# Mixture of experts: ranking the experts right behind the router's mask, and spreading the 64-slot blocks among the 128-slot blocks

## The chip, the cores and the metric

The kernel runs on one core of a Trainium2 chip. The metric is the device time in microseconds of one execution. One execution was recorded by the hardware profiler; times inside it are counted from the start of its span.

## The reference

The model is a chain of three blocks on a sequence of 256 tokens with 1024 channels, all in float32. What comes last, and takes almost half of the time, is the feed-forward part of the third block, a mixture of 8 experts of which each token uses two:

```python
def moe_swiglu(h, router, we_gate, we_up, we_down):
    logits = (h @ router).astype(jnp.float32)
    top_v, top_i = lax.top_k(logits, TOP_K)
    top_w = jax.nn.softmax(top_v, axis=-1)
    gates = jnp.sum(jax.nn.one_hot(top_i, N_EXPERTS, dtype=jnp.float32) * top_w[..., None], axis=-2)
    out = jnp.zeros_like(h)
    for e in range(N_EXPERTS):
        out = out + gates[..., e:e + 1] * swiglu(h, we_gate[e], we_up[e], we_down[e])
    return out
```

`swiglu` is `(silu(h @ w_gate) * (h @ w_up)) @ w_down`, with 1024 x 3584 for gate and up and 3584 x 1024 for down. Three float32 matrices for each of 8 experts are 352 MB, and every one is read from HBM once. The result is added to the residual stream x, which is the kernel's output. The two blocks before, and the attention of the third, are untouched by the change.

## The kernel before

**Slots.** The kernel doesn't run all 256 tokens through each expert. It has eight places for experts, numbered by `KINDS`, with a fixed number of slots each: the places 0, 2 and 4 (kind F) have 128, the places 1, 3, 5, 6 and 7 (kind N) have 64. `route` (from L1310) computes the logits, finds each token's two experts, and builds `mask` (L1354), a 0/1 matrix of tokens by experts. Two sums over it follow on TensorE: `pos` (L1362, L1363), each token's position in its expert's queue, and `cnt` (L1398, L1399, in `count`), each expert's number of tokens. `one_hots` (L1477, four instructions) compares positions with slot numbers and so makes the selection matrix `sel` of a group, and `gather` (L1500) multiplies the tokens by it, so that the chosen tokens stand in the slots. For kind F the operands are split into a high and a low part (`hth`, `htl`, L268 and L269), for three matmuls with rounded operands instead of one in full float32.

**Ranking.** `order` ranks experts 1 to 7 by count on VectorE, and so decides which expert takes which place: the fullest get 128 slots. Place 0 is always expert 0. It writes `ids` as integers into `self.ci` (L1427), the largest overflow likewise (L1433), and the positions `spos` sorted by place (L1441 and L1442 in `sort`). SyncE loads the ids into registers (L1644, `values_load`), because the address of a weight tile depends on them; it loads the overflow (L1646), which says at the end whether a second round is needed. With the inputs here none is run.

**Blocks.** Each expert's 3584 hidden channels are worked on in 7 blocks of 512. A block loads six tiles of 1 MB: two of gate, two of up, two of down. All loads are issued by SyncE in the order of the program, each into a buffer of a ring: 10 buffers and 2 more, and 3 further ones until the third block. A load has to wait until the tile that was in its buffer has been read. In a block of kind F each tile is split by ScalarE (`whi`, L305) and VectorE (`wlo`, L306) in two halves of 1024 columns, into four buffers of each, and is free when that is done, and TensorE runs 24 matmuls of 512 columns for each of gate, up and down (L1566, L1589). In a block of kind N the raw tile goes to TensorE in float32 (L1558, 16 matmuls of 256 columns for each of gate and up; L1577, 8 of 512 for down), and is free when those have run. The down part of a block is run behind the gate and up parts of the next. After an expert's last block, `combine` scales its result (`yh` on ScalarE, `yl` on VectorE, L1678 and L1679), multiplies by the transposed selection (`cmb`), and adds to x on VectorE: 8 additions of 128 x 256 for N (L1688), 4 of 128 x 512 for F (L914). The program (`experts`, from L1592) makes a list `seq` of 56 blocks; before, with e0 to e7 the places, it is

- F F, then N F nineteen times, then N sixteen times.

The gather for the next group of `GROUPS` stands two or three blocks ahead of its first block. Within the engines a scheduler may move instructions by priority; each engine then runs its own list in order.

Of the kernel before, what the change touches and what calls it, by code (L numbers as in the profile page):

```python
# [24 lines left out]
SWA_ORDER = [0, 3, 1, 4, 2, 5, 6, 9, 7, 10, 8, 11]  # L25
CAP = {"F": 128, "N": 64}
KINDS = "FNFNFNNN"
GROUPS = ((0,), (1,), (2, 3), (4, 5), (6,), (7,))
TAGS = ("u", "u", "x2", "u", "x2", "u")
HEAD = 2  # L30
PE_TAPS = 13
EARLY = 7
# [3 lines left out]
AHEAD = 3  # L36
# [172 lines left out]
class Build:  # L209
# [1102 lines left out]
    def route(self):  # L1312

        nc = self.nc
        t = self.units(4, "hn")
        self.ht = []
        after = self.after  # L1320
        acc = self.sum_sq(self.x[:3], fold=False)
        with self.tc.high_priority(offset=400):
            pl = self.pa("router")
            for j in range(4):
                for c in range(2):
                    g = self.col("swf_g", 2 * j + c)
                    if (j, c) == (3, 1):
                        nc.vector.tensor_scalar(t[j][:, c, :], self.x[j][:, c, :], g, None, op0=OP.mult)
                    else:
                        hn = nc.scalar.activation(t[j][:, c, :], self.x[j][:, c, :], AF.Copy, scale=g)  # L1330
                for c in range(2):
                    cc = 2 * j + c
                    for tb in range(2):
                        mm = nc.tensor.matmul(pl[:, tb * 8:(tb + 1) * 8], t[j][:, c, tb * 128:(tb + 1) * 128],
                                              self.col("router", cc * 8, 8), start=cc == 0 and tb == 0, stop=cc == 7,
                                              skip_group_check=True)
            rt = self.cpool.tile([128, 160], F32, name="rt")
            two = lambda o, w: rt[:, o:o + 2 * w].rearrange("p (a b) -> p a b", a=2)
            first = lambda m, k: m[:, :, k:k + 1].to_broadcast([128, 2, 8])
            lg, mx, ixf = rt[:, 0:16], two(16, 8), two(32, 8)  # L1340
            mask, tmp, pos = rt[:, 48:64], two(64, 8), rt[:, 80:96]
            ix = self.mpool.tile([128, 16], U32, name="ix", tag="m")
            nc.vector.tensor_copy(lg, pl[:, 0:16])
            for tb in range(2):
                s = slice(tb * 8, tb * 8 + 8)
                nc.vector.max(mx[:, tb, :], lg[:, s])
                nc.vector.max_index(ix[:, s], mx[:, tb, :], lg[:, s])
            nc.vector.tensor_copy(rt[:, 32:48], ix)
            iota = self.con("iota", 0, 8).rearrange("p (a b) -> p a b", a=1).to_broadcast([128, 2, 8])
            hot = two(112, 8)  # L1350
            m3 = mask.rearrange("p (a b) -> p a b", a=2)
            nc.vector.tensor_tensor(hot, iota, first(ixf, 0), op=OP.is_equal)
            nc.vector.tensor_tensor(tmp, iota, first(ixf, 1), op=OP.is_equal)
            masked = nc.vector.tensor_tensor(m3, hot, tmp, op=OP.add)  # L1354
            pt = []
            with after(mm):
                for j in range(4):
                    pt.append(self.turn(t[j], "PSSP"[j]))
            for j in range(HT0):
                self.turned(pt[j], masked, hn)  # L1360
            pp = self.pa("pos")
            nc.tensor.matmul(pp[:, 0:16], self.con("before"), mask, start=True, stop=False, skip_group_check=True)  # L1362
            nc.tensor.matmul(pp[:, 8:16], self.con("one").to_broadcast([128, 128]), mask[:, 0:8], start=False, stop=True,  # L1363
                             skip_group_check=True)
            nc.vector.scalar_tensor_tensor(pos, pp[:, 0:16], 1.0, mask, op0=OP.add, op1=OP.mult)
            self.pos, self.rt = pos, rt
            self.count()
            sel = self.one_hots(0, 0)
            for j in range(HT0, 4):
                self.turned(pt[j], self.hots, hn)  # L1370
            nxt = self.gather(0, sel, tags="ASP")
            self.order()
        with after(*self.gathered):
            rc = self.rms_col(self.sum_sq(self.x[3:], acc=acc))
            d, gw = two(96, 1), two(98, 2)
            nc.vector.tensor_tensor(d, mx[:, :, 1:2], mx[:, :, 0:1], op=OP.subtract)
            nc.vector.tensor_tensor(d, d, rc.rearrange("p (a b) -> p a b", a=2), op=OP.mult)
            nc.scalar.activation(gw[:, :, 1:2], d, AF.Exp)
            nc.vector.tensor_scalar(d, gw[:, :, 1:2], 1.0, None, op0=OP.add)
            nc.vector.reciprocal(gw[:, :, 0:1], d)  # L1380
            nc.vector.tensor_tensor(gw[:, :, 1:2], gw[:, :, 1:2], gw[:, :, 0:1], op=OP.mult)
            nc.vector.tensor_tensor(hot, hot, first(gw, 0), op=OP.mult)
            nc.vector.tensor_tensor(tmp, tmp, first(gw, 1), op=OP.mult)
            gates = two(128, 9)
            nc.vector.tensor_tensor(gates[:, :, 0:8], hot, tmp, op=OP.add)
            nc.vector.tensor_copy(gates[:, :, 8:9], rc.rearrange("p (a b) -> p a b", a=2))
            self.gates = gates
        for tb in range(2):
            self.sort(self.sgates[:, tb, 0:8], gates[:, tb, 0:8])
        nc.vector.tensor_copy(self.sgates[:, :, 8:9], gates[:, :, 8:9])  # L1390
        return nxt
# [9 lines left out]
    def order(self):  # L1401


        nc = self.nc
        pc = self.pc
        so = self.unit("so").rearrange("p a b -> p (a b)")
        cnt, key, rank = so[:, 0:8], so[:, 8:16], so[:, 16:24]
# [13 lines left out]
        nc.vector.tensor_tensor(P, each(so[:, 202:210], 8), row(rank, 8), op=OP.is_equal)  # L1421

        self.order_of = P, t
        ids, over = so[:, 186:194], so[:, 194:202]
        self.sort(ids, self.con("iota", 0, 8))
        self.ci = so[:, 211:220].bitcast(I32)
        nc.vector.tensor_copy(self.ci[:, 0:8], ids)  # L1427
        self.sort(over, cnt)
        ends = over.rearrange("p (a b) -> p a b", b=2)
        nc.vector.tensor_scalar(ends[:, 0:3, 0:1], ends[:, 0:3, 0:1], float(CAP["N"] - CAP["F"]), None, op0=OP.add)  # L1430
        nc.vector.tensor_reduce(so[:, 210:211], over, axis=AX.X, op=OP.max)
# [49 lines left out]
    def gather(self, g, sel, tag="u", tags="A"):  # L1481

        nc = self.nc
        kinds = [KINDS[e] for e in GROUPS[g]]
        xe = {}
# [106 lines left out]
    def experts(self, rnd, nxt):  # L1592


        nc = self.nc
        blocks = {k: [(e, b) for e in range(8) if KINDS[e] == k for b in range(7)] for k in "FN"}
        seq = blocks["F"][:HEAD]
        for n, f in zip(blocks["N"], blocks["F"][HEAD:]):
            seq += [n, f]
        seq += blocks["N"][len(blocks["F"]) - HEAD:]  # L1600
        at = {group[0]: g for g, group in enumerate(GROUPS)}
        early = {seq.index((group[0], 0)) - (2 if g == 1 else AHEAD): g for g, group in enumerate(GROUPS) if g}
        back, state, xes, yps, done = {}, {0: nxt}, {}, {}, None
        last, self.queued = None, []
        if rnd == 0:
# [1 line left out]
        for i, (e, b) in enumerate(seq):  # L1607
# [31 lines left out]
            if i in early:  # L1639
                g = early[i]  # L1640
# [75 lines left out]
```

## Time and profile before

| | us |
|---|---|
| median of 3 runs (lowest, highest) | 1842.62 (1842.45, 1848.72) |
| profiled execution, its own time | 1842.34 |
| its span | 1840.6 |
| TensorE busy (share of the span) | 1777.9 (97%) |
| VectorE busy | 1105.8 (60%) |
| ScalarE busy | 876.8 (48%) |
| mean DMA rate | 289 GB/s |

The span begins with the first instruction and ends with the last; the execution's own time is 1.7 us longer. The shares are means over stages that differ much: the routing starts at about 983 us, the first expert's matmuls at 995.9 us, the last load lands at about 1827 us. The page's chain of waits names only the final addition into x (L1688), so that what bounds the end has to be read from windows and timelines of the stages.

### The profile page before, as it was taken

What the parts mean: (1) busy time and instruction counts of PE and PEld (TensorE: products, weight loads), DVE (VectorE), ACT (ScalarE), POOL (GpSimd) and SP (SyncE); (2) the same over time, 40 slices, a digit from 0 to 9 for tenths busy, and PEclk for the clock granted to TensorE, in tenths of its full rate; (3) what the DMA queues carried; (4) which work ended last, traced back from release to release, by engine and by line L of the source; (5) the groups of instructions that cost most, each with busy time, mean ns of one, the idle gap of its engine ahead of it and who ended that gap; (6) DMA issues with size and microseconds to landing.
All of it is one profiled execution on the core that took longest, in us unless ns stands there. A gap on an engine that the chain in (4) does not pass through costs nothing. (4 is left out here: it accounts for less than half of the span.)

```text
span 1840.6 us, 30697 instructions
## 1 busy us (share of the span) xinstructions
PE 1777.9 (97%) x12370; PEld 1449.9 (79%) x12370; DVE 1105.8 (60%) x1730; ACT 876.8 (48%) x1345; POOL 11.4 (1%) x31
## 2 busy tenths in 40 slices
PE   7999999999999999999999999999999999999886
PEld 7989999989999979999978766666676667655432
DVE  7689788766467977665687754566565646420100
ACT  5545555555455675454576644545454545410000
POOL 0000000000000000000000000000000000000000
PEclk9999999999999999999998999999999999999999
DMA  9766468445554315555635899999999999999997
GB/s 307 250 247 229 166 233 296 149 150 198 191 185 165 115 46 196 191 176 180 244 115 196 353 397 420 420 415 418 421 421 414 416 408 420 420 420 420 421 420 298
DMA packets 77654, 531.30 MB, mean 289 GB/s; under 512 B 9282, under 2 KB 10050, under 8 KB 15424
## 3 DMA queue, kind: packets, MB, share of 16 engines
q1 hardware_dynamic: 75168, 524.66, 72.9%
q0 software_dynamic: 1328, 3.29, 0.9%
q8 instruction: 99, 1.62, 0.4%
q10 hardware_dynamic: 1008, 1.31, 0.2%
q14 instruction: 51, 0.42, 0.1%
HBM read 526.60 MB, written 2.62 MB: 288 GB/s over the span
## 5 line engine op out<-in xcount | busy, mean ns | idle before, releaser
L306 DVE TENSOR_TENSOR wlo<-raw,whi 128x1024 fp32r<-128x1024 f32 (+1 forms) x534 | 630.4, 1203 | 288.9 <-ACT whi L305 287.1
L305 ACT ACTIVATE whi<-raw 128x1024 fp32r<-128x1024 f32 (+1 forms) x534 | 543.3, 1040 | 355.1 <-PE lin L325 236.5
L325 PE MATMUL lin<-hh,whi 128*128 128x256 f32 x1248 | 355.6, 285 | 10.3 <-ACT whi L305 8.1
L325 PE MATMUL lin<-hl,whi 128*128 128x256 f32 x1248 | 354.3, 284 | 0.3
L325 PE MATMUL lin<-hh,wlo 128*128 128x256 f32 x1248 | 352.7, 283 | 1.8 <-DVE wlo L306 1.8
L325 PEld LDWEIGHTS lin<-hh,whi 128*128 128x128 f32 x1248 | 237.7, 191 | 14.5 <-ACT whi L305 9.1
L325 PEld LDWEIGHTS lin<-hh,wlo 128*128 128x128 f32 x1248 | 237.2, 190 | 4.7 <-DVE wlo L306 2.5
L325 PEld LDWEIGHTS lin<-hl,whi 128*128 128x128 f32 x1248 | 237.8, 191 | 2.4 <-issue 1.0
L1577 PE MATMUL y<-raw,an 128*64 128x512 f32 x560 | 131.3, 600 | 9.5 <-DMA raw<-we_down 9.0
L1558 PE MATMUL up<-raw,xn 128*64 128x256 f32 x1120 | 130.6, 381 | 9.3 <-DMA raw<-we_up 5.5
L1636 DVE SCALAR_TENSOR_TENSOR act<-up,gs,act 128x256 f32<-128x256 f32 (+1 forms) x56 | 32.6, 583 | 173.1 <-PE up L1558 142.0
L1558 PE MATMUL g<-raw,xn 128*64 128x256 f32 x1120 | 130.8, 383 | 5.8 <-DMA raw<-we_gate 5.8
L1558 PEld LDWEIGHTS up<-raw,xn 128*64 128x64 f32 x1120 | 80.0, 137 | 54.0 <-ACT act L289 8.2
L1558 PEld LDWEIGHTS g<-raw,xn 128*64 128x64 f32 x1120 | 76.6, 137 | 49.6 <-DMA raw<-we_gate 10.8
L1566 PE MATMUL g<-whi,xe 128*128 128x512 f32 x336 | 106.4, 398 | 0.0
L1566 PE MATMUL up<-whi,xe 128*128 128x512 f32 x336 | 104.7, 393 | 0.0
L1577 PEld LDWEIGHTS y<-raw,an 128*64 128x64 f32 x560 | 37.2, 136 | 82.7 <-issue 64.2
L289 ACT ACTIVATE act<-g,gs 128x256 f32<-128x256 f32 (+1 forms) x56 | 31.0, 554 | 126.2 <-PE g L1558 106.1
L1665 ACT ACTIVATE an<-aT 128x256 f32<-128x256 f32 x35 | 13.4, 382 | 146.5 <-PE aT L1662 146.5
L1566 PEld LDWEIGHTS up<-whi,xe 128*128 128x128 f32 x336 | 63.2, 188 | 13.9
L325 PE MATMUL ff<-fl,whi 128*128 128x256 f32 x256 | 71.8, 281 | 0.0
L325 PE MATMUL ff<-fh,wlo 128*128 128x256 f32 x256 | 71.8, 281 | 0.0
(457 smaller groups left out, 3082.6 us busy)
## 6 DMA issues: line engine op xcount, KB each, us to landing
raw<-we_gate SPq DMA_DIRECT2D x112, 1024.0 KB, 11.5
raw<-we_up SPq DMA_DIRECT2D x112, 1024.0 KB, 12.0
raw<-we_down SPq DMA_DIRECT2D x112, 1024.0 KB, 12.5
raw<-w_in SPq DMA_DIRECT2D x35, 1024.0 KB, 6.2
raw<-w_ff SPq DMA_DIRECT2D x32, 1024.0 KB, 4.9
raw<-ada_w SPq DMA_DIRECT2D x24, 1024.0 KB, 5.3
raw<-cv_w_gate SPq DMA_DIRECT2D x11, 1024.0 KB, 4.8
raw<-cv_w_up SPq DMA_DIRECT2D x11, 1024.0 KB, 4.8
```

The lines of the kernel that those rows point to most:

```text
L289: self.last_gate = self.nc.scalar.activation(*args, **kw)
L305: self.splits_done.append(nc.scalar.activation(hi[:, :w], raw[:, o:o + w], AF.Copy))
L306: self.low_done = nc.vector.tensor_tensor(lo[:, :w], raw[:, o:o + w], hi[:, :w].bitcast(F32), op=OP.subtract)
L325: nc.tensor.matmul(o, s, m, start=start and n == 0, stop=stop and n == 2, skip_group_check=True)
L1558: nc.tensor.matmul(ps[64 * h:64 * h + 64, 0:256], xe["N"][:, kk, :], raw[:, k * 512 + h * 256:k * 512 + (h + 1) * 256], start=kk == 0, sto ...
L1566: nc.tensor.matmul(ps, s, m, start=n == 0, stop=n == 23)
L1577: self.downs = nc.tensor.matmul(yp[0][64 * n:64 * n + 64, :], st, raw[:, k * 1024 + n * 512:k * 1024 + (n + 1) * 512], start=b == 0 and pa ...
L1636: nc.vector.scalar_tensor_tensor(t, pu[:, 0:w], gs[1], t, op0=OP.mult, op1=OP.mult)
L1665: nc.scalar.activation(an[:, 0:256], pt[:, 0:256], AF.Copy)
```

## The change

`route` now calls `count` and `order` right behind the mask, ahead of the transposes of the tokens and of the matmuls for `pos`. The second half of `order` becomes `overflow`: the sort of the counts, the largest overflow, and the sorts of the positions (`spos`); it is called behind the first `gather`. In `experts` the list of blocks is now made by spreading the 19 F blocks that follow the first two evenly over 35 N blocks:

- F F, then sixteen times N N F and three times N F among them, the last of these at the end. The last block is so of kind F (e4); before it was N (e7).

Place 5 is now gathered before and apart from place 4, which makes one more gather in all; a group is gathered ahead of whichever of its experts comes first in the list.

```diff
--- before.py
+++ after.py
@@ -25,8 +25,8 @@
 SWA_ORDER = [0, 3, 1, 4, 2, 5, 6, 9, 7, 10, 8, 11]
 CAP = {"F": 128, "N": 64}
 KINDS = "FNFNFNNN"
-GROUPS = ((0,), (1,), (2, 3), (4, 5), (6,), (7,))
-TAGS = ("u", "u", "x2", "u", "x2", "u")
+GROUPS = ((0,), (1,), (2, 3), (5,), (4,), (6,), (7,))
+TAGS = ("u", "u", "x2", "u", "u", "x2", "u")
 HEAD = 2
 PE_TAPS = 13
 EARLY = 7
@@ -1352,6 +1352,9 @@
             nc.vector.tensor_tensor(hot, iota, first(ixf, 0), op=OP.is_equal)
             nc.vector.tensor_tensor(tmp, iota, first(ixf, 1), op=OP.is_equal)
             masked = nc.vector.tensor_tensor(m3, hot, tmp, op=OP.add)
+            self.rt = rt
+            self.count()
+            self.order()
             pt = []
             with after(mm):
                 for j in range(4):
@@ -1363,13 +1366,12 @@
             nc.tensor.matmul(pp[:, 8:16], self.con("one").to_broadcast([128, 128]), mask[:, 0:8], start=False, stop=True,
                              skip_group_check=True)
             nc.vector.scalar_tensor_tensor(pos, pp[:, 0:16], 1.0, mask, op0=OP.add, op1=OP.mult)
-            self.pos, self.rt = pos, rt
-            self.count()
+            self.pos = pos
             sel = self.one_hots(0, 0)
             for j in range(HT0, 4):
                 self.turned(pt[j], self.hots, hn)
             nxt = self.gather(0, sel, tags="ASP")
-            self.order()
+            self.overflow()
         with after(*self.gathered):
             rc = self.rms_col(self.sum_sq(self.x[3:], acc=acc))
             d, gw = two(96, 1), two(98, 2)
@@ -1421,11 +1423,16 @@
         nc.vector.tensor_tensor(P, each(so[:, 202:210], 8), row(rank, 8), op=OP.is_equal)
 
         self.order_of = P, t
-        ids, over = so[:, 186:194], so[:, 194:202]
+        self.so, ids = so, so[:, 186:194]
         self.sort(ids, self.con("iota", 0, 8))
         self.ci = so[:, 211:220].bitcast(I32)
         nc.vector.tensor_copy(self.ci[:, 0:8], ids)
-        self.sort(over, cnt)
+
+    def overflow(self):
+
+        nc = self.nc
+        so, over = self.so, self.so[:, 194:202]
+        self.sort(over, so[:, 0:8])
         ends = over.rearrange("p (a b) -> p a b", b=2)
         nc.vector.tensor_scalar(ends[:, 0:3, 0:1], ends[:, 0:3, 0:1], float(CAP["N"] - CAP["F"]), None, op0=OP.add)
         nc.vector.tensor_reduce(so[:, 210:211], over, axis=AX.X, op=OP.max)
@@ -1595,11 +1602,16 @@
         nc = self.nc
         blocks = {k: [(e, b) for e in range(8) if KINDS[e] == k for b in range(7)] for k in "FN"}
         seq = blocks["F"][:HEAD]
-        for n, f in zip(blocks["N"], blocks["F"][HEAD:]):
-            seq += [n, f]
-        seq += blocks["N"][len(blocks["F"]) - HEAD:]
-        at = {group[0]: g for g, group in enumerate(GROUPS)}
-        early = {seq.index((group[0], 0)) - (2 if g == 1 else AHEAD): g for g, group in enumerate(GROUPS) if g}
+        rest = blocks["F"][HEAD:]
+        for n, block in enumerate(blocks["N"]):
+            seq.append(block)
+            k = len(rest) * (n + 1) // len(blocks["N"]) - len(rest) * n // len(blocks["N"])
+            seq += rest[len(seq) - n - 1 - HEAD:][:k]
+        assert len(seq) == 56
+        at = {}
+        for g, group in enumerate(GROUPS):
+            at[min(group, key=lambda e: seq.index((e, 0)))] = g
+        early = {seq.index((e, 0)) - (2 if g == 1 else AHEAD): g for e, g in at.items() if g}
         back, state, xes, yps, done = {}, {0: nxt}, {}, {}, None
         last, self.queued = None, []
         if rnd == 0:
```

The order of VectorE's instructions between the mask (L1354) and the gather. `cnt`, `pos` are the sums, `so` holds all of the ranking, `sel` is the selection, `htl` the low part of the transposed tokens, `xe` the gathered ones. Before:

```order
L1354 TENSOR_TENSOR rt<-rt 128x16
L269 TENSOR_TENSOR htl<-ht,hth 128x512
L1365 SCALAR_TENSOR_TENSOR rt<-pos,rt 128x16
L1477 TENSOR_SCALAR sel<-consts,rt 128x128 x4
L269 TENSOR_TENSOR htl<-ht,hth 128x512 x3
L1510 CAST xe<-xe 128x256 x3
L1410 COPY so<-cnt 128x8
```

And now, from the row behind the mask on:

```order
L1412 COPY so<-cnt 128x8
L1368 SCALAR_TENSOR_TENSOR rt<-pos,rt 128x16
L1413 SCALAR_TENSOR_TENSOR so<-so,consts 128x8
L1417 TENSOR_TENSOR so<-so 128x7x7
L269 TENSOR_TENSOR htl<-ht,hth 128x512
L1419 TENSOR_REDUCE so<-so 128x7
L1484 TENSOR_SCALAR sel<-consts,rt 128x128
L1423 TENSOR_TENSOR so<-so 128x64
L1484 TENSOR_SCALAR sel<-consts,rt 128x128
L1448 TENSOR_TENSOR so<-so,consts 128x64
L1484 TENSOR_SCALAR sel<-consts,rt 128x128
L1449 TENSOR_REDUCE so<-so 128x8
```

The fourth `sel` and the conversion of the ids (L1429) come next, and then three `htl`. Ranking and selection now stand interleaved, where the ranking stood behind three of the gather's conversions; on TensorE the two matmuls of `cnt` have changed places with those of `pos`.

SyncE's queue around the first load of the ids (L1644 before, L1656 now); `raw` is a tile of weights. Before:

```order
L281 DMA raw<-we_up 128x2048 x2
L281 DMA raw<-we_down 128x2048 x3
L281 DMA raw<-we_gate 128x2048
L1644 TENSOR_LOAD so
L1644 ISA x2
```

And now:

```order
L281 DMA raw<-we_up 128x2048 x2
L281 DMA raw<-we_down 128x2048 x3
L1656 TENSOR_LOAD so
L1656 ISA x2
L281 ISA
```

One load of gate, which belonged to the fourth block (expert 0, whose address is known) stood ahead of the ids; the fourth block is now of kind N, and its loads come behind.

VectorE's last rows; `al` is the low part of the activations, `cmb` the combined result. Before:

```order
L1636 SCALAR_TENSOR_TENSOR act<-up,gs,act 128x256 x5
L1679 SCALAR_TENSOR_TENSOR yl<-y_16641,gs,yh 128x512
L1688 TENSOR_TENSOR x<-x,cmb 128x256 x8
L1646 TENSOR_LOAD so
L1303 COMPARE_AND_BRANCH
```

And now:

```order
L306 TENSOR_TENSOR wlo<-raw,whi 128x1024 x8
L1648 SCALAR_TENSOR_TENSOR act<-up,gs,act 128x512
L1691 SCALAR_TENSOR_TENSOR yl<-y_16041,gs,yh 128x512
L1681 TENSOR_TENSOR al<-aT,ah 128x512
L1700 TENSOR_TENSOR x<-x,cmb 128x256 x8
L306 TENSOR_TENSOR wlo<-raw,whi 128x1024 x4
L1691 SCALAR_TENSOR_TENSOR yl<-y_15279,gs,yh 128x512
L914 TENSOR_TENSOR x<-x,cmb 128x512 x2
L1691 SCALAR_TENSOR_TENSOR yl<-y_15280,gs,yh 128x512
L914 TENSOR_TENSOR x<-x,cmb 128x512 x2
```

The list ended with one result to scale and eight additions; it now ends with those of e7, the splits of the last two down tiles of e4 behind them, and then the two results of e4 with four additions of twice the size.

## Rows read from the trace of the kernel before

**Rows 1.** The second part of the page: the span in 40 slices of 46 us, one digit or number per slice. Busy tenths of TensorE, and GB/s moved.

```profile
PE   7999999999999999999999999999999999999886
GB/s 307 250 247 229 166 233 296 149 150 198 191 185 165 115 46 196 191 176 180 244 115 196 353 397 420 420 415 418 421 421 414 416 408 420 420 420 420 421 420 298
```

**Rows 2.** Busy time by window. Columns: the window in us from the span's start, its length, busy us of PE, PEld, DVE, ACT and POOL with the number of instructions in brackets, granted TensorE clock (1.00 is 2.4 GHz, 0.50 is 1.2 GHz), DMA share, GB/s. First four stages in order, then three short windows inside the third.

```profile
984.00:1000.00 16.00, 16.00 (x84) 15.31 (x84) 10.69 (x43) 7.05 (x14) 0.52 (x1) 0.68 0.20 67
1032.00:1064.00 32.00, 32.00 (x192) 21.88 (x190) 19.05 (x22) 15.57 (x19) 0.53 (x1) 1.00 0.80 293
1064.00:1600.00 536.00, 532.37 (x2977) 368.96 (x2972) 301.29 (x326) 254.42 (x315) 1.58 (x3) 1.00 1.01 417
1600.00:1816.00 216.00, 193.64 (x1366) 103.24 (x1366) 25.04 (x51) 22.46 (x48) 0.00 (x0) 1.00 1.01 420
1208.00:1216.00 8.00, 8.00 (x60) 4.21 (x58) 1.10 (x2) 1.40 (x3) 0.00 (x0) 1.00 0.98 386
1414.00:1434.00 20.00, 20.00 (x122) 12.29 (x122) 10.56 (x14) 7.24 (x9) 0.00 (x0) 1.00 0.98 393
1478.00:1490.00 12.00, 12.00 (x85) 6.75 (x85) 2.67 (x4) 2.84 (x4) 0.00 (x0) 1.00 0.98 369
```

**Rows 3.** Who SyncE's DMA queue waited for: first between 976 and 1004 us, then (behind the dots) between 1195 and 1210 us. Total us, times, longest.

```profile
SPq L1644 <- DVE so L1441: 13.8, 1, 13.8
...
SPq L281 <- DVE wlo L306: 10.6, 3, 5.3
```

**Rows 4.** Timeline of the DMA issues on SyncE's queue. Columns: start, us until the last issue of the row has been made, line, tile and source, number of issues.

```profile
984.36 0.33 SPq L281 DMA_DIRECT2D raw<-we_gate  x1
999.43 0.90 SPq L281 DMA_DIRECT2D raw<-we_gate  x2
1044.53 3.08 SPq L281 DMA_DIRECT2D raw<-we_gate  x2
1050.23 3.11 SPq L281 DMA_DIRECT2D raw<-we_up  x2
1058.36 2.06 SPq L281 DMA_DIRECT2D raw<-we_down  x2
1062.54 0.91 SPq L281 DMA_DIRECT2D raw<-we_gate  x2
```

**Rows 5.** Timeline of TensorE: the first gate matmuls of a 128-slot block (L1566), and of the 64-slot blocks of two later pairs (L1558). Columns: start, us, line, tiles, shapes, number.

```profile
1045.04 0.71 PE L1566 MATMUL g<-whi,xe 128*128 128x512 f32 x2
1088.87 3.67 PE L1558 MATMUL g<-raw,xn 128*64 128x256 f32 x32
1117.19 1.08 PE L1558 MATMUL g<-raw,xn 128*64 128x256 f32 x8
```

**Rows 6.** Timeline around the router's mask and the ranking, VectorE first, then TensorE. Columns as in rows 5; in square brackets the idle time before and what ended it.

```profile
986.35 0.17 DVE L1354 TENSOR_TENSOR rt<-rt 128x16 f32<-128x16 f32 x1
989.18 0.17 DVE L1365 SCALAR_TENSOR_TENSOR rt<-pos,rt 128x16 f32<-128x16 f32 x1 [1.89 <-PE pos L1363]
989.40 0.87 DVE L1477 TENSOR_SCALAR sel<-consts,rt 128x128 fp32r<-128x128 f32 x4
995.49 0.15 DVE L1410 COPY so<-cnt 128x8 f32<-128x8 f32 x1
997.93 0.22 DVE L1442 TENSOR_REDUCE so<-so 128x8 f32<-128x64 f32 x1
998.19 0.17 DVE L1427 CAST so<-so 128x8 int32<-128x8 f32 x1
988.29 0.45 PE L1362 MATMUL pos<-rt,consts 128*128 128x16 f32 x2
989.43 0.57 PE L1399 MATMUL cnt<-rt,consts 128*128 128x8 f32 x2
995.89 0.63 PE L1566 MATMUL g<-whi,xe 128*128 128x512 f32 x2
```

**Rows 7.** Busy time by windows of 1 us around the routing; columns as in rows 2.

```profile
982.00:983.00 1.00, 0.04 (x1) 0.00 (x0) 0.89 (x2) 0.98 (x2) 0.00 (x0) 1.00 0.00 0
984.00:985.00 1.00, 1.00 (x7) 1.00 (x7) 0.34 (x1) 0.00 (x0) 0.00 (x0) 0.51 0.00 0
994.00:995.00 1.00, 1.00 (x9) 1.00 (x9) 0.42 (x1) 0.32 (x2) 0.00 (x0) 0.87 0.00 0
995.00:996.00 1.00, 1.00 (x10) 1.00 (x10) 0.85 (x7) 0.72 (x4) 0.00 (x0) 1.00 0.08 16
```

**Rows 8.** Timeline of the end of the span: the last down matmuls, the two halves of the scaled result, and the eight additions into x.

```profile
1827.29 1.94 PE L1577 MATMUL y<-raw,an 128*64 128x512 f32 x8 [0.17 <-DMA raw<-we_down]
1829.27 0.69 ACT L1678 ACTIVATE yh<-y,gs 128x512 fp32r<-128x512 f32 x1 [4.14 <-PE y L1577]
1829.99 0.75 DVE L1679 SCALAR_TENSOR_TENSOR yl<-y,gs,yh 128x512 fp32r<-128x512 f32 x1 [10.09 <-ACT yh L1678]
1831.33 2.74 DVE L1688 TENSOR_TENSOR x<-x,cmb 128x256 f32<-128x256 f32 x8 [0.59 <-PE cmb L1684]
```

**Rows 9.** Groups of instructions by line and shape between 1064 and 1620 us: count | busy us, mean ns of one | idle time before, and what ended it.

```profile
L306 DVE TENSOR_TENSOR wlo<-raw,whi 128x1024 fp32r<-128x1024 f32 x216 | 253.1, 1222 | 98.2 <-ACT whi L305 97.3
L914 DVE TENSOR_TENSOR x<-x,cmb 128x512 f32<-128x512 f32 x8 | 5.3, 682 | 2.0 <-PE cmb L1695 2.0
```

## The prediction

> **What bounds the kernel now.** I read the page's slices first, then windows by stage, then SyncE's waits and issues, since the page's chain ends at once. In the slices the last eighteen move about 420 GB/s whatever TensorE does [rows 1]. The windows say the same by stage: 417 GB/s from 1064 to 1600 us, while TensorE is busy 532 of 536 us, and 420 from 1600 to 1816, while it is idle 216.0 - 193.6 = 22.4 us [rows 2]. The reader is to see that 420 is a ceiling: the rate is no higher where TensorE waits for data. A load of 1 MB (1.049 MB decimal) is then 2.5 us, six for a block 15.0 us. What can be gained in the experts is DMA time below 420, and it lies in three places: a gap at 984 to 1000 us (67 GB/s), 1032 to 1064 (293), and some dips behind 1064 [rows 2].
>
> The gap has a named cause: SyncE waits 13.8 us for the ranking before it can address expert place 1 [rows 3], between the issues at 984.4 and 999.4 us [rows 4]. The second shortage and the dips are waits for ring buffers: the loads issued from 1044.5 on come one by one as buffers come free [rows 4], and during the dip at 1208 SyncE waited for splits, at most 5.3 us at a time [rows 3]. TensorE meanwhile never stops. An N-F pair takes it 1117.19 - 1088.87 = 28.3 us [rows 5]; an N block is three parts of 3.67 us and a transpose, 11.3, so an F block is 17.0. So at the start TensorE is behind the loads and frees the buffers late; the early part is paced by TensorE, the rest by DMA.
>
> **The ranking moved.** `cnt` now runs where `pos` ran, and `pos` where `cnt` ran, which ended at 989.43 + 0.57 = 990.0 us, where `pos` was read at 989.18 [rows 6]. So the positions come 0.8 us later. Behind them VectorE has six operations of the ranking and one `htl` (0.69) among the four selections. The small ones hold 0.17 to 0.22 us each; I take 0.13 from start to start, as they overlap, and 0.26, the step from 997.93 to 998.19 [rows 6], as the upper bound. Selections end at 990.0 + 0.17 + 0.69 + 6 x 0.13 + 0.87 = 992.5 us, against 990.27: TensorE's gather, and with it the first gate matmul (995.89), is 2.2 us late, at most 3.0. The ids are converted at about 992.7 instead of 998.2, 5.5 us early, and SyncE's loads leave at 994 instead of 999.4.
>
> What is that worth? Those five loads fill buffers that are free anyway; the first of them is needed by the third block, whose matmuls begin behind 1030 us. The buffers after them come free by TensorE's progress. So I cost the earlier ids at nothing, and the late gather in full. The load that stood ahead of the ids (984.36 [rows 4]) now stands behind them and behind the load of the overflow, which waits for the first gather; its buffer is free, and it is needed behind 1045 us.
>
> The clock adds to that. TensorE stood still from 982 to 983.5 us, ran at 0.51 from 984 on, and was granted 1.00 again at 995, ten us later [rows 7]. Now it also stands still for some 2 us around 991, while the clock is half. By how much that puts off the return no row shows: not at all, or at worst by ten us from the new start at 992.4, to 1002.5; work that ran at full clock from 996.3 on would then lose (1002.5 - 996.3) / 2 = 3.1 us. I take 1.0, nearer to nothing, as the gap lies in a stretch that is slow already.
>
> **The blocks spread, early part.** The fourth block was F and began at 1045.04 us [rows 5]. The loads that reuse the buffers of that block left at 1044.5, 1047, 1050 and 1053 us, and the next four from 1058.4 to 1063; from that fifth load on DMA never lacked one [rows 4]. Now the fourth block is N. It begins at 1045.0 + 2.2, and frees a buffer each 3.67 / 2 = 1.84 us: the first at 1049.1, and faster than the 2.5 us that a load takes. So DMA is full from the first of these loads on, and the fifth begins at 1049.1 + 4 x 2.5 = 1059.1 instead of 1058.4: the stream is 0.7 us late (1.7 with the clock). Without the late gather it would be 1.5 us early. Three blocks N N F then take TensorE 39.6 us where their loads take 45.0, so that it gains on the loads steadily.
>
> **The blocks spread, later part.** From 1064 to 1600 the mean of 417 is short of 420 by 536 x 3 / 420 = 3.8 us. Three dips hold 0.65 + 1.29 + 1.46 = 3.4 of it [rows 2]. They come where a gather or a combine is added to a pair that leaves TensorE only 30.0 - 28.3 us. With N N F it has 5.4 us in three blocks, and I take the 3.4 as won; the bounds are 0 and 3.8. The one more gather (32 matmuls, about 6 us of TensorE) hides in 22 us of idle time that it has to the end.
>
> The Trainium skill (Perfetto Trace Analysis, Optimization Strategy) says that a kernel whose most contended engine changes between regimes may gain by interleaving them. Here the windows bear out the two regimes for TensorE, and only 3.8 us for DMA. By the page's rule the gain would be up to TensorE's idle time in the second regime; that is the third rival below.
>
> **The end.** Before, the last load was used at 1827.29 us (T), N's matmuls took 1.94, and behind them came `yh`, `yl`, a wait of 0.59 and eight additions to 1834.07 [rows 8], T + 6.8. Now the last load is F's. Its eight last tiles are g, g, u, u of e4, two down tiles of e7, two of e4, each 2.5 us apart, the first at T - 17.5. TensorE is behind an F block's splits and can take it up at about T - 16; gate and up take two thirds of 17.0, e7's down matmuls 3.6, so that these end at Y = T - 0.5. Then, as before, `yh` to the last of eight additions takes 4.84 us (Y + 4.9, with `al` in the wait). The four splits of e4's down tiles stand behind these additions on VectorE: 4 x 1.22 [rows 9], to Y + 9.8. TensorE's last matmul 0.4, `yh` 0.69, `yl` 0.75, the wait 0.6, two additions 1.36 [rows 9], `yl` 0.75, wait 0.6, two additions 1.36: Y + 16.3 = T + 15.8. The end is 9.0 us longer; bounds 6.5, if Y comes when e7's last tile has landed (T - 3), and 12, if TensorE comes one F tile (2.9) late. Storing x takes as long as before.
>
> **The sum.** 0.7 + 1.0 - 3.4 + 9.0 = 7.3 us on the profiled execution's 1842.34: 1849.6 us. That execution stands 0.3 us below the median of 1842.62.
>
> **The rivals.**
> - *The clock stays low (slower).* If the pause at 991 keeps TensorE at half clock through the first block's gate and up, 11.4 us of work, these take twice that from where the clock came back: some 6 us in place of my 1.0, all of it in the paced start. 1842.3 + 12.3 = 1854.6. For it: ten us of half clock behind a pause of 1.5 us [rows 7]. Against: TensorE is busy at both sides of the new pause. It decides, with a total over 0.5%, from about 3 us on. The Trainium skill (TensorE: Matmul & The Clock Gate, HAM oscillation) says that idle gaps bring the clock down again and again, and the cost is the slow stretch behind each; here the row at 984 agrees for one gap.
> - *The dips remain (slower).* If they are not TensorE's, or the added gather makes new ones, 3.4 us aren't won: 1853.0. Against: at 1600 to 1816 there are none.
> - *The wait for the ids was the start's bound (no change).* If loads 5.5 us earlier carry through, the start gives 5.5 instead of costing 1.7: 1842.4. For it: 13.8 us of named wait and 67 GB/s. Against: TensorE doesn't stand still behind 1000 us.
> - *The regimes even out (faster).* If the mixed stretch was held by TensorE and not by 420, most of the 22.4 us of idle time comes back: 1842.3 + 1.7 - 22.4 + 9.0 = 1830.6. Against: 417 of 420.
>
> **How the numbers follow.** Forecast 0.50, of which 0.05 lies above the bound; clock 0.15; dips 0.10; ids 0.20; regimes 0.05. A measurement of this kernel can tell 0.5%, 9.2 us, from no change: below 1833.4 is faster, above 1851.8 slower. Faster 0.05; slower 0.05 + 0.15 + 0.10 = 0.30; same 0.65. The range leaves out the regimes and the upper tail of the clock: 1841.5 to 1855. The forecast's own range is 1846 to 1853.
>
> **What would show it.** First gate matmul 2.2 to 3.2 us later against the end of the attention; the wait for the ids short by some 5 us; no slot waits behind 1064 and 420 GB/s throughout; TensorE's idle time spread over the last 500 us; the last load about 2 us earlier; from it to the last addition 15.8 us, the four last splits behind the eight additions. The forecast is wrong if the last load lands more than 5 us off, or if the end is under 12 us.

## The result, and the profile after

The changed kernel takes 1862.67 us (median of 4 runs, 1861.60 to 1865.81), against 1843.92 for the kernel before on the same chip: a ratio of 1.0111, 95% interval 1.0092 to 1.0130. The ratios here and below are estimated over the fast runs of both kernels and aren't the quotients of the medians (1.0102 here). It is slower by 19 us (medians) to 20.5 us (ratio); I had forecast 1849.6, with 1855 as the upper end. The profiled execution took 1861.96 us, its span is 1860.2.

That span can be taken apart. The attention's last matmul ends at 982.0 us before and at 984.5 now, in a part that the change doesn't touch (it ends between 981.8 and 987.9 us in all the profiles of this study). Its row before, its row now, and the first gate matmul now:

```profile
981.76 0.28 PE L325 MATMUL lin<-oah,wlo 128*128 128x256 f32 x1
...
984.17 0.28 PE L325 MATMUL lin<-oah,wlo 128*128 128x256 f32 x1
998.89 0.62 PE L1573 MATMUL g<-whi,xe 128*128 128x512 f32 x2
```

From there to the end of the span it is 858.6 us before and 875.8 now, +17.2. In what follows this is called the stage time; it is read from one profiled execution of each kernel, while the ratios rest on several. It is made of three pieces, which the rows give.

First the windows of the changed kernel that answer to [rows 2], same columns:

```profile
1032.00:1064.00 32.00, 32.00 (x213) 21.37 (x213) 13.42 (x18) 12.38 (x16) 0.52 (x1) 1.00 0.74 292
1064.00:1600.00 536.00, 515.62 (x3076) 337.10 (x3076) 230.37 (x275) 191.42 (x256) 1.58 (x3) 0.99 1.01 420
1600.00:1816.00 216.00, 204.75 (x1215) 130.68 (x1212) 83.16 (x91) 73.54 (x96) 0.00 (x0) 0.98 1.01 417
```

From 1064 to 1600 us the loads now run at 420 GB/s where they ran at 417: the dips there are gone. Behind 1600 us it is 417 where it was 420. Their end, from the DMA view of 1815 to 1830 us in 40 slices of 0.375 us (GB/s in each; the end is known to a slice), is at slice 27, 1825.1 us:

```profile
GB/s 415 437 437 415 393 415 437 437 415 393 415 437 459 393 415 393 437 459 393 415 437 393 306 153 131 131 109 0 0 0 0 0 0 0 0 44 0 0 0 0
```

Before, the same view ends at slice 31, 1826.6 us:

```profile
GB/s 481 371 437 393 459 437 371 437 393 481 415 350 437 393 415 437 371 437 415 415 350 262 284 240 262 240 218 218 131 44 22 0 0 0 0 0 0 0 0 0
```

Behind the end of the attention the last byte lands 840.7 us late now, 844.6 before: 3.9 us are won there. But TensorE is no longer level with the loads when they end. The end of the span, TensorE first, then VectorE, answers to [rows 8]:

```profile
1832.81 3.65 PE L1584 MATMUL y<-raw,an 128*64 128x512 f32 x16
1842.51 0.73 PE L1596 MATMUL y<-wlo,ah 128*128 128x512 f32 x2 [2.10 <-DVE wlo L306]
1844.10 1.05 PE L1596 MATMUL y<-wlo,ah 128*128 128x512 f32 x2
...
1837.24 0.75 DVE L1691 SCALAR_TENSOR_TENSOR yl<-y,gs,yh 128x512 fp32r<-128x512 f32 x1 [3.56 <-ACT yh L1690]
1837.90 0.68 DVE L1681 TENSOR_TENSOR al<-aT,ah 128x512 fp32r<-128x512 f32 x1
1838.58 2.74 DVE L1700 TENSOR_TENSOR x<-x,cmb 128x256 f32<-128x256 f32 x8
1841.23 4.63 DVE L306 TENSOR_TENSOR wlo<-raw,whi 128x1024 fp32r<-128x1024 f32 x4
1849.02 0.75 DVE L1691 SCALAR_TENSOR_TENSOR yl<-y,gs,yh 128x512 fp32r<-128x512 f32 x1 [3.16 <-ACT yh L1690]
...
1853.14 1.28 DVE L914 TENSOR_TENSOR x<-x,cmb 128x512 f32<-128x512 f32 x2 [0.71 <-PE cmb L1707]
```

e7's last down matmuls end at 1836.46 us (Y), 11.3 us behind the last byte; from Y to the last addition, 1854.42, it is 18.0 us. Last byte to last addition is 29.3 us where it was 7.4. So: -3.9 + 21.9, less 0.8 for a shorter store, is +17.2. The whole loss is at the end, and a little over half of it is that TensorE arrives there late; the rest is the 128-slot block that now stands last.

The profile of before has a slow start: its first gate matmul comes 13.9 us behind the attention's end, and 11.2 in the four other profiles with its routing. As an estimate from the pairs of runs below, some 2 of these 2.7 us reach the end, so that against a usual execution the loss in stage time is some 19 us, as by the medians.

Why it is late stands in TensorE's waits from 1064 to 1836 us (total us, times, longest), all of them:

```profile
PE g L1573 <- ACT whi L305: 20.8, 14, 1.6
PE g L1573 <- DVE wlo L306: 7.9, 16, 0.5
PE y L1596 <- DVE wlo L306: 2.5, 2, 1.3
PE up L1565 <- DVE gs L1547: 0.3, 1, 0.3
PE xe L1507 <- ACT xn L1520: 0.2, 1, 0.2
```

No load is among them. It waits 14 times for ScalarE's split of a gate tile, 28.7 us with VectorE's half (the second row). One of these places, ScalarE first, then TensorE:

```profile
1223.85 0.47 ACT L289 ACTIVATE act<-g,gs 128x256 f32<-128x256 f32 x1 [3.23 <-PE g L1565]
1231.15 0.38 ACT L1677 ACTIVATE an<-aT 128x256 f32<-128x256 f32 x1 [6.83 <-PE aT L1674]
1231.43 5.79 ACT L305 ACTIVATE whi<-raw 128x1024 fp32r<-128x1024 f32 x6
...
1230.62 0.44 PE L1674 MATMUL aT<-consts,act 128*128 128x128 f32 x2
1232.53 0.73 PE L1573 MATMUL g<-whi,xe 128*128 128x512 f32 x2 [1.48 <-ACT whi L305]
1233.79 0.50 PE L1573 MATMUL g<-wlo,xe 128*128 128x512 f32 x1 [0.53 <-DVE wlo L306]
```

ScalarE stands idle for 6.83 us with the split next but one in its list: ahead of it stands `an`, the copy of the second N block's activations, whose transposes `aT` TensorE runs last before the F block. Only then come `an` and the split, and TensorE has nothing to do. In the kernel before, F always followed a single N, and such a place reads:

```profile
1251.39 1.06 ACT L305 ACTIVATE whi<-raw 128x1024 fp32r<-128x1024 f32 x1 [3.77 <-issue]
1253.05 1.07 ACT L305 ACTIVATE whi<-raw 128x1024 fp32r<-128x1024 f32 x1 [0.60 <-PE y L1589]
1256.49 0.39 ACT L1665 ACTIVATE an<-aT 128x256 f32<-128x256 f32 x1 [2.37 <-PE aT L1662]
...
1256.07 0.38 PE L1662 MATMUL aT<-consts,act 128*128 128x128 f32 x2
1256.21 0.71 PE L1566 MATMUL g<-whi,xe 128*128 128x512 f32 x2
```

There the two splits of the first gate tile stand ahead of `an`, and the matmuls follow the transposes without a gap. The Trainium skill (TensorE: Matmul & The Clock Gate, the section "Architectural detail: the array is 16× 32×32, not 1× 128×128") says that ScalarE's and VectorE's queues are strictly first in, first out; these rows agree.

### The profile page after: what moved, and what is told of

The parts are those of the page before. It is cut to its first block, busy times and chain, and to the rows that moved or that the text cites. A ratio compares the mean times of both kernels' runs of the same rounds, so it can differ in the third digit from the quotient of the medians.

```text
span 1860.2 us, 30740 instructions
## 1 busy us (share of the span) xinstructions
PE 1793.7 (96%) x12402; PEld 1464.4 (79%) x12402; DVE 1106.7 (59%) x1734; ACT 874.0 (47%) x1345; POOL 11.4 (1%) x31
## 5 line engine op out<-in xcount | busy, mean ns | idle before, releaser
L1573 PE MATMUL g<-whi,xe 128*128 128x512 f32 x336 | 112.3, 417 | 20.8 <-ACT whi L305 20.8
L1573 PEld LDWEIGHTS g<-whi,xe 128*128 128x128 f32 x336 | 65.2, 199 | 37.2 <-ACT whi L305 24.1
L1573 PE MATMUL g<-wlo,xe 128*128 128x512 f32 x168 | 71.0, 423 | 7.9 <-DVE wlo L306 7.9
```

Source lines behind the costliest of these rows:

```text
L1573: nc.tensor.matmul(ps, s, m, start=n == 0, stop=n == 23)
```

## The experiments

Theory A: these late splits, all along the mixed stretch, keep TensorE behind the loads. Theory B: the last block alone makes the loss. Theory C: the added gather does, with the clock. Theory D: the moved ranking does. Ratios below are to the kernel before on the same chip, with 95% intervals. In the cuts of code, three dots stand for lines left out.

**The splits moved ahead, and moved back.** In the first run the changed kernel loads and splits the first gate tile of an F block that follows two N ahead of `an` (`ahead_of` is true there, and `TILES` is 1):

```diff
+            if ahead_of(seq, i):
+                n, m = seq[i + 1]
+                for part in range(TILES):
+                    raw = self.load_w(self.weights("we_gate", n, 2 * m + part))
+                    self.ready["we_gate", n, m, part] = self.split_w(raw, 2048)
+                    self.behind += self.splits_done
             act = self.act_split(e, t)
...
-                nc.scalar.activation(an[:, 0:256], pt[:, 0:256], AF.Copy)
+                with self.after(*self.behind):
+                    nc.scalar.activation(an[:, 0:256], pt[:, 0:256], AF.Copy)
```

> The changed kernel, but where a 128-slot block follows two 64-slot blocks, ScalarE's two splits of its first gate tile stand ahead of the copy of the second 64-slot block's activations, and no longer behind it. Theory A (late splits): in the trace of the changed kernel TensorE waits 28.7 us in all for these splits (20.8 for the high parts, 7.9 for the low), all in blocks of 128 slots behind two of 64, and so never catches up with the loads; its gate and up end some 10 us behind the last load. Without them it catches up: the waits fall below 8 us, and the end comes 8 to 12 us earlier, 1851 to 1855 us. Theory B (the last block alone, two more results and four splits behind the additions): no change, 1861 to 1865. Theory C (the added gather and the slow clock make the lag): no change either, since neither is touched.

Measured: 1849.24 us, ratio 1.0040 (1.0022 to 1.0059); stage time 865.0. That is 10.8 us of stage time under the changed kernel, as A said, with the same number of instructions on TensorE, VectorE and ScalarE. TensorE's waits for gate splits fell less than I expected, from 28.7 to 12.8 us:

```profile
PE g L1574 <- ACT whi L305: 6.7, 5, 1.4
PE g L1574 <- DVE wlo L306: 6.1, 12, 1.4
PE y L1597 <- DVE wlo L306: 4.6, 3, 2.1
PE y L1597 <- ACT whi L305: 4.5, 3, 1.7
PE y L1585 <- DMA raw<-we_down: 3.3, 6, 0.6
```

but many are of another kind: loads are among them, and at three of the five gate tiles where TensorE still waits for ScalarE, ScalarE waits for the load (at the two others, the splits stand behind `yh` of an expert that has just ended). The last of the three, and Y's matmuls:

```profile
1776.23 2.01 ACT L305 ACTIVATE whi<-raw 128x1024 fp32r<-128x1024 f32 x2 [9.09 <-DMA raw<-we_gate]
1819.66 3.65 PE L1585 MATMUL y<-raw,an 128*64 128x512 f32 x16
```

TensorE is level with the loads, and Y is 1823.31, 0.4 us behind the last byte (1822.9 in this run).

In the second run the kernel before gets the order that hurts: its splits of the first gate tile are put behind `an`.

```diff
-            w = self.split_w(raw, 2048)
+            with self.after(*self.behind):
+                w = self.split_w(raw, 2048)
+            self.behind = []
...
             act = self.act_split(e, t)
+            self.behind = [self.an] if kind == "N" else []
```

> The kernel before, but with the splits of each 128-slot block's first gate tile put behind the copy of the 64-slot block ahead of it on ScalarE, as they stand in the changed kernel behind two 64-slot blocks. Theory A: each of 19 such blocks costs TensorE 1.3 to 2 us more at its start, in a stretch where a pair of blocks has only 1.7 us to spare, so that TensorE holds the loads up: 15 to 38 us longer, 1859 to 1882, with waits of TensorE for splits of 20 us or more and less than 410 GB/s between 1064 and 1600 us. Theories B and C: the place of the splits on ScalarE is of no matter, 1842 to 1846.

Measured: 1882.18 us, ratio 1.0198 (1.0170 to 1.0226), some 37 us; stage time 898.6, +40.0. The first of its waits, and its mixed stretch:

```profile
PE g L1568 <- ACT whi L305: 23.4, 17, 1.5
...
1064.00:1600.00 536.00, 503.20 (x2762) 341.74 (x2759) 275.31 (x301) 228.46 (x287) 1.05 (x2) 0.99 0.97 387
```

A pair of blocks without a gather takes 1308.00 - 1277.33 = 30.7 us there, 2.4 more than the 28.3 of [rows 5], and 17 times 2.4 is about the 40 us. TensorE then holds up the loads, 387 GB/s. So the order on ScalarE's list, with the same instructions, is shown to cost this, in both directions; B and C can't explain either run.

**The two halves of the change apart.**

> The change's routing alone (ranking right behind the mask, slot sort behind the first gather), with the list of blocks and the groups of before. Theory A: the start is worth within 2 us either way, 1842 to 1846. Theory D (the moved ranking makes the loss, by the late first gather and the clock): most of the 19 us, 1855 or more. If the earlier ids were worth what they save in SyncE's wait, 1838 to 1840.

> The change's list of blocks and groups alone, with the routing of before. Theories A, B and C: the whole loss is here, 1860 to 1866. Theory D: 1842 to 1850.

The routing alone: 1845.55 us, ratio 1.0017 (1.0000 to 1.0035). The list alone: 1860.43 us, ratio 1.0087 (1.0067 to 1.0106). D falls; the loss is the list's. What the routing costs shows better where all else is equal: the changed kernel has 2.0 us more of stage time than the list alone (873.7), and in two more such pairs below it is 2.4 and 2.5. Each is a difference of two single executions; the three agree, and the ratios of all three pairs point the same way.

**The tail.** First the last two blocks were exchanged, so that the list ends in F F N, without and with the early splits, and then with the routing of before as well:

```diff
+        seq[-2:] = seq[:-3:-1]
```

> The changed kernel with the last two blocks of the list exchanged, so that it ends with a block of 64 slots, as before. Theory A (late splits all along, TensorE some 10 us behind the loads at the end): the lag stays, only the two results of the last 128-slot block and their four splits no longer stand alone at the end; by the timeline of the changed kernel TensorE's last down matmuls would end at about 1843 us and the last addition 5 us later, 1847.5 instead of 1854.4: 1853 to 1858 us. Theory B (the last block alone makes the loss): the end is 6.8 us behind the last load again, 1838 to 1845.

> Both repairs on the changed kernel: the splits of the first gate tile ahead of the copy where a 128-slot block follows two of 64, and a 64-slot block at the end. Theory A: TensorE is level with the loads, as in the run with the early splits alone, and the end is 7 us behind the last load instead of 18: 11 us under that run, 1836 to 1842 us, level with the kernel before or up to 4 us under it. If the loss were a lag that the late splits only add to, 1845 or more would remain.

> As the run with both repairs, but with the routing of before, so that only the list of blocks is changed. Theory A, with the routing's move costing the start 1 to 3 us (1.0017 of before when it was made alone): 1 to 3 us under the run with both repairs, 1834 to 1840 us. If the earlier ids are worth something once DMA alone sets the pace, 1 to 4 us over it.

All three missed: 1.0125 (1.0097 to 1.0152), 1.0059 (1.0036 to 1.0081) and 1.0028 (1.0008 to 1.0049); stage times 876.1, 865.0 and 862.5, so that the exchange alone gains nothing. I had moved the F block away from the end and made F F of it. Two F take TensorE 34 us by the 17.0 of the prediction, where their loads take 30, and of the down matmuls the second F's in part and all of the last N's still come behind the last load. The comparison of the last two, 2.4 us of stage time for the routing, holds.

Then the last eleven blocks were put in the order N F N N F N F N F N N, which has two N at the end and no F F:

```diff
+        tail = {k: [s for s in seq[-11:] if KINDS[s[0]] == k] for k in "FN"}
+        seq[-11:] = [tail[k].pop(0) for k in "NFNNFNFNFNN"]
```

> The changed kernel with its last eleven blocks reordered to N F N N F N F N F N N, so that two blocks of 64 slots end the list and no two of 128 stand together. The run with the last two exchanged ended in F F N, where TensorE has to do more behind the last load; this end is the one of before. Theory A (a lag of some 10 us by the late splits all along): the tail behind the last load is cut by the results and splits of the last 128-slot block, about 11 us, but most of the lag stays: 1.003 to 1.008 of before. Theory B (the last block alone): level with before or under it, 0.996 to 1.000. If only TensorE's sum of work counts, the order at the end is of no matter and the ratio stays at 1.010 to 1.012.

> The same list with the splits of the first gate tile ahead of the copy. Theory A: TensorE is level with the loads, the last load lands some 4.7 us earlier behind the end of the attention than before, and the last addition comes 6.8 us behind it instead of 18.5: 11 us under the run with the early splits alone, 0.996 to 0.999 of before. If the end isn't shortened by the order of the last blocks, 1.003 to 1.005.

> The same with the routing of before. Theory A with the moved ranking costing the start some 2.4 us: 0.995 to 0.998 of before, the fastest of all. If the routing is of no matter, level with the run before it.

Measured, without the early splits, with them, and with them and the routing of before: 1.0071 (1.0052 to 1.0091), 0.9990 (0.9980 to 1.0000) and 0.9985 (0.9974 to 0.9996); stage times 867.7, 855.4 and 852.9. Of the second, the end:

```profile
1824.84 3.65 PE L1585 MATMUL y<-raw,an 128*64 128x512 f32 x16 [0.47 <-ACT an L1691]
1830.60 2.74 DVE L1714 TENSOR_TENSOR x<-x,cmb 128x256 f32<-128x256 f32 x8 [0.59 <-PE cmb L1710]
```

The last addition is at 1833.34, 8.2 us behind the last byte (1825.1). The two causes are so measured apart: from 875.8 us of stage time the early splits take 10.8, and the end in two N a further 9.6; both together take 20.4, and what is left is 3.2 us under the kernel before. Made alone, the new end takes 8.1, but not all of that is the end: the new order has only 12 late splits in place of 14, with 24.7 us of waits in place of 28.7. The first two runs lie within the ranges expected by A. The third, at 1838.93 us the fastest of all, lies 0.15% below the kernel before and a little above its range, and its ratio isn't told from that of the second.

**The order at the end of VectorE's list.** The run with the early splits, with the last four splits ahead of the eight additions, which are held behind them:

```diff
-            if done:
+            if done and i + 1 < len(seq):
                 self.combine(*done)
...
-        if done:
-            self.combine(*done)
         self.down_proj(last[0], last[2], act, yps[last[0]])
+        if done:
+            self.combine(*done, behind=[self.low_done])
```

> The run with the early splits (list ending in a 128-slot block), and at the end the four last splits on VectorE and the last down matmuls on TensorE stand ahead of the eight additions of the expert that ends one block earlier. In the run with the early splits TensorE's last down matmuls wait 2.1 us for these splits, which begin when the additions are done, 4.8 us after its activations are ready. Theory A: the end is 3 to 5 us shorter, 1844 to 1847 us. If the wait is covered by other work, no change: 1848 to 1851.

Measured: 1849.53 us, ratio 1.0035 (1.0015 to 1.0056), not told from the run it starts from. In the profile the piece from Y (1825.15) to the last addition (1840.25) did fall from 18.0 to 15.1 us, but Y came 2.4 us later behind the end of the attention in this execution, in which the clock was down at two more places. What the order is worth stays open.

**One gather less.** Places 4 and 5 gathered together again:

```diff
-GROUPS = ((0,), (1,), (2, 3), (5,), (4,), (6,), (7,))
-TAGS = ("u", "u", "x2", "u", "u", "x2", "u")
+GROUPS = ((0,), (1,), (2, 3), (4, 5), (6,), (7,))
+TAGS = ("u", "u", "x2", "u", "x2", "u")
```

> The changed kernel with places 4 and 5 gathered together, as before: one gather less, 32 matmuls and some 6 us of TensorE. Theory A: TensorE never waits for a load in the changed kernel, so what it is spared it is ahead at the end: 4 to 7 us under the changed kernel, 1.007 to 1.009 of before. My prediction's reading, that a gather hides in idle time: no change, 1.010 to 1.012. Theory C (the gather alone makes the lag): 1.000 to 1.003.

Measured: 1862.10 us, ratio 1.0104 (1.0084 to 1.0123), stage time 878.1: no gain that can be told, and A missed. The ratio is the one expected of a gather that hides in idle time, but TensorE waits for no load here either. What the profiled execution shows is the clock; among the four it is the longest and has the lowest mean clock, 0.981 (the others 0.983 to 0.985, the changed kernel's 0.983 to 0.986). The same windows as above:

```profile
1064.00:1600.00 536.00, 514.86 (x3032) 336.45 (x3031) 229.63 (x271) 191.15 (x256) 1.57 (x3) 0.98 1.01 419
1600.00:1816.00 216.00, 204.63 (x1199) 130.92 (x1199) 81.04 (x89) 70.77 (x93) 0.00 (x0) 0.97 1.01 412
```

In windows of 4 us the granted clock falls to 0.6 or 0.7 at ten F blocks here and at five in the changed kernel, and at none in the kernel before. One of the five, where each pair of gate matmuls takes 1.05 us in place of 0.62:

```profile
1790.77 0.74 PE L1573 MATMUL g<-whi,xe 128*128 128x512 f32 x2 [1.48 <-ACT whi L305]
...
1793.38 1.05 PE L1573 MATMUL g<-whi,xe 128*128 128x512 f32 x2
```

Such a gate part lasts 8.2 us, and 6.6 where the clock stays up: 1.6 us each, so five more of them give back 8 us, about what a gather takes (some 6) and the 2.3 us by which the stage is longer. Why the clock fell in ten blocks here and in five there, with the same waits ahead of it, these runs don't tell, nor whether the missing gather has to do with it: one execution of each was profiled.

## Why the prediction was wrong

The step that failed is the one in "The end": "TensorE is behind an F block's splits and can take it up at about T - 16 ... so that these end at Y = T - 0.5", and with it, in "The blocks spread, early part", "it gains on the loads steadily".

- **Y.** Predicted half a us before the last load is used, which before was 0.7 us behind the last byte; so 0.2 us behind that, and measured 11.3. (The terms as written, T - 16, two thirds of 17.0 and 3.6, give T - 1.1 and not T - 0.5; these 0.6 us are not what failed.) My 39.6 us for N N F was the sum of blocks read in the old order, where no split was late. A triple of the changed kernel without a gather or a combine takes 41.7 us (1207.14 to 1248.82), and 1.6 more where the clock falls. With gathers and combines on top, that left TensorE too little to catch up with. With the splits early, Y came 0.4 us behind the last byte, as forecast: the reckoning was right for a kernel with the splits on time. That this run's profiled 1849.04 us is so near the forecast of 1849.6 is in part luck, since the errors below, from Y on and in the loads, cancel. I had looked at VectorE's and SyncE's lists, and not at ScalarE's.
- **From Y on.** Predicted 16.3 us, measured 18.0 in the changed kernel and in the run with early splits. The mechanism is the one named, four splits behind eight additions; the size was 1.7 short. The last split ends at Y + 9.4 (9.8 in the sum), and from the first `yh`, at 1848.30, to the end it is 6.1 us, as in the sum. Between them TensorE's down matmuls ran at a granted clock of 0.51 from 1843.8 to 1847.1 us, behind their wait of 2.10 us, and a pair of them took 1.05 us in place of 0.73: half of 3.3 us is the 1.7. The sum had no term for it.
- **Dips.** Predicted 3.4 us won, with no dips behind 1064; the rate is 420 there. With the start, the last load was to be 1.7 us earlier (0.7 + 1.0 - 3.4) and is 3.9. In the prediction's terms the list was to win 1.5 + 3.4 and the routing to cost 2.2 + 1.0. The list alone has its last byte 840.8 us behind the attention's end, the routing alone 844.7, the kernel before 844.6: the list wins 3.8, and the routing's cost doesn't show in the last load here (with the splits early it does, by 2.4 and 2.7).
- **Routing.** Predicted, against no move, 2.2 us for the late gather and 1.0 for the clock. The first gate matmul starts 14.4 us behind the end of the attention in the changed kernel (14.3 to 14.8 in all runs of the new routing), and 11.2 in four runs of the old one: 3.2 us, of which 2.0 to 2.5 reach the end. But the profile of before itself had 13.9, since its clock stayed at 0.5 for ten us [rows 7], and only for some 3.4 us in the other runs of the old routing; so the routing alone shows just 0.2 us of stage time against that profile. The ids' loads left 7 us earlier behind the attention's end and were worth nothing, as said.
- **The clock rival.** Part of it is true: the new pause brings a second slow stretch. These are windows of 2 us of the changed kernel, columns as in [rows 2]; the clock is at 0.50 in the first, back in the second and third, and at 0.50 again in the fourth, behind TensorE's pause:

```profile
988.00:990.00 2.00, 2.00 (x11) 2.00 (x10) 0.47 (x4) 1.49 (x3) 0.00 (x0) 0.50 0.00 0
990.00:992.00 2.00, 1.24 (x10) 1.15 (x8) 0.85 (x5) 0.64 (x2) 0.52 (x1) 0.87 0.00 0
992.00:994.00 2.00, 1.18 (x6) 0.83 (x7) 2.00 (x11) 0.00 (x0) 0.00 (x0) 0.99 0.00 0
994.00:996.00 2.00, 2.00 (x11) 2.00 (x11) 1.53 (x3) 0.77 (x2) 0.00 (x0) 0.50 0.35 49
996.00:998.00 2.00, 2.00 (x14) 2.00 (x13) 0.98 (x3) 0.33 (x2) 0.00 (x0) 0.66 0.72 279
```

- **The regimes even out.** As I had worked out the rule on interleaving (the Trainium skill, Perfetto Trace Analysis, Optimization Strategy), it would have given up to 22.4 us; this is the fourth of my rivals, where the text calls it the third. With both faults mended, the best run has 5.7 us of stage time less than the kernel before, some 2 of which are the slow start in that one's profile; by the ratio it is 2.8. 420 GB/s was the bound, as [rows 2] said: that run moves 420 GB/s from 1064 to 1600 us and 419 from 1600 to 1816. ([rows 1] show that rate in the fifteen slices from the 25th to the 39th, not in all of the last eighteen.)
- **The extra gather** was to hide in the time in which TensorE waits for loads. There was none in the changed kernel; taking the gather out gained nothing that can be told all the same, with a lower clock.

On the profiled execution the forecast missed by 12.4 us: 11.2 by Y, 1.7 from Y to the last addition and 2.4 by an attention that ended later, less 2.2 by the loads and 0.8 by the store; the rest is rounding. None of my rivals was this one; the three tenths for slower stood on other mechanisms. Nor did the two signs of being wrong that I had named cover it: the last load was 2.2 us off, and an end that is too long, 29.3 us behind the last byte where 16.5 was forecast, was not among them.

## What to carry to other kernels

When the order of work on the bound engine changes, read the new order on every engine that prepares its operands: an engine that works its list in order can have the next block's operands ready in memory and still stand behind a copy that the bound engine itself releases last. A time for a group of blocks taken from one order holds for another only if what stands ahead of the preparation stays the same. And what comes last in the list should be the kind of block with the least work behind its last load, without putting two heavy ones in front of it.

## What the runs showed of the hardware

A wait of TensorE of 1.4 to 1.6 us, with 0.4 or 0.5 more right behind it, was followed by half the clock for some 3.4 us in five of the fourteen F blocks of the changed kernel that have it, in ten of fourteen with one gather less, and in two of seventeen in the kernel before with the late order forced on it; in the others with the same wait the clock stayed up. At the end of the changed kernel a wait of 2.1 us was followed by 3.3 us at 0.51. The Trainium skill (TensorE: Matmul & The Clock Gate, HAM oscillation) tells of gaps that bring the clock down again and again; these rows agree for a part of the gaps, and that it happens behind gaps as short as this I had not expected. And work taken off TensorE need not come back as time: in the profile with one gather less, the mean clock from 1600 to 1816 us was 0.97 in place of 0.98, and nothing was gained.
